# One decoder layer on one core: the last merge's gate blocks as paired half-block products, two groups of copies moved ahead, a shorter head norm

## The chip, the cores and the metric

One of the eight cores of a Trainium2 chip runs the whole program. The metric is the device time of one execution in microseconds; lower is better. TensorE (PE) multiplies, VectorE (DVE) and ScalarE (ACT) do elementwise work, GpSimd (POOL) does a few small steps, SyncE (SP) issues the DMAs.

## What is computed

One layer of a hybrid decoder for 512 prompt tokens and 32 sample tokens (8 sequences of 4), 544 columns in all, with 1024 channels, in float32. Cut to what matters here:

```python
h = rmsnorm(x)
z = h @ w_in                      # conv inputs, q, k, v, o, and three merge gates g_a, g_b, g_c
y_c = (sigmoid(o) * headnorm(mlstm(q, k, v))) @ w_out_c     # 4 heads of 256, RMS norm per head
y_a = (b * dwconv3(c * x_a)) @ w_out_a
y_b = silu(layernorm(dwconv31(glu))) @ w_out_b
u = sigmoid(g_a) * y_a + sigmoid(g_b) * y_b + sigmoid(g_c) * y_c
x = x + u @ w_o
x = x + cross_attention(rmsnorm(x), keys and values of 256 memory tokens)   # p_mem_k, p_mem_v are outputs too
x = x + (silu(gate) * up) @ w_ffn_out
```

## The kernel before

**Numbers in two parts.** Every float32 operand of a large product is split into a rounded high part (ACT copy) and the rest (DVE subtract), `split`, L112; a product is three passes, high by high, high by low and low by high (`PASSES`). Activations lie as channels by tokens in eight tiles of 128 x 544. The 544 columns are worked in two halves of 272 (`HN`), one PSUM bank each.

**Blocks.** `block` makes 128 output channels: for each of the input tiles k, three passes and two halves, so a block of `w_in` with 8 input tiles is 48 matmuls of 128x128 by 272 columns and a block of `w_out_b` with 4 input tiles is 24. The order of TensorE's instructions is the order of the code (`manual_schedule` for PE); on the other engines and on the DMA queue a scheduler orders instructions by a priority, which is their place in the program, PE's instructions counted. `evacuate` moves what it emits 150 places ahead, the weight loads 300 (`PRIO`), `urgent` 600. Weights stream in the order of the list `order`, `ahead` blocks in advance: a DMA to a `wr` buffer (4), a split into a `w` buffer (3).

**Stages.** Queries, keys, values and output gates of the four heads, with the memory's keys and values (`mem_k`, `mem_v`) and the heads' attention put between the matmuls as hooks; then the convolution inputs; then three merges of eight pairs of blocks: gates 68 to 75 with `w_out_c`, 52 to 59 with `w_out_a`, 60 to 67 with `w_out_b` (`merge`, L1038). Then `w_o` and the residual, cross attention, and the feed-forward part. The PSUM has eight banks; `psum(name, mm, s1)` gives mm tiles of two banks and s1 tiles of one.

**The places that the change touches.**
- `merge`: gate block (48 matmuls), Sigmoid into `sg`, `w_out` block (24 matmuls), `sg *= y`, `u[j] += sg`; in the last merge `u[j]` is also split into a pair of an `act` buffer (20 of them).
- `s_pair` (L1483, with `product`, L1474) is how most of the feed-forward part is already done: two blocks of 8 input tiles, taken as a two by two scheme of 512 input channels by 272 columns, come from seven half-block products instead of eight (12 matmuls each) of sums of weights and sums of activations. Its operands are `sA` to `sE` (weights and their sums, `s_emit`) and `b11`, `b2`, `n1t3`, `n2t4` (`b_forms`). Its PSUM tiles `sy` (2), `sz`, `sx` are one bank each.
- `mem_v` (L526): value products of the memory, half by half, into two one-bank tiles that the second half releases by an ACT copy with a scale, `vo`; `mem_rows` (L517) needs a one-bank tile for two transposes (L388).
- `numer` and `finish` (L845, L886): numerator, its sum of squares, and the head norm in [128, 5] columns; POOL makes the power -1/2 (L900); five scalings of `num` (L99) precede the transposes of `head_out` (L911).
- Cross attention: `mqx` and `pm`, zeroed by POOL (L121) when the pool of phase x opens; `xs_t` (L1264) transposes the probabilities and splits them. A pool of a later phase can reuse memory that a closed one has given back.
- `wide_rsqrt` (L346) for the layer norm.

Of the kernel before, what the change touches and what calls it, by code (L numbers as in the profile page):

```python
# [15 lines left out]
P = 128  # L16
# [19 lines left out]
def layer(ctx: ExitStack, tc: tile.TileContext, a):  # L36
# [122 lines left out]
        order += [("in", 4 + c), ("in", 8 + c), ("in", c)]  # L159
    for j in range(8):  # L160
        order += [("in", 52 + j), ("oa", j)]
    for j in range(8):
        order += [("in", 60 + j), ("ob", j)]
    order += [("o", j) for j in range(8)]
    order += [("xq", j) for j in range(8)]
    order += [("xo", j, hf) for hf in range(2) for j in range(8)]
# [21 lines left out]
    def w_emit(key, parts=1):  # L188

        if key[0][0] == "s":  # L190
            with tc.high_priority(PRIO):
                return s_emit(*key)
        if key[0] == "fo":
            return fo_emit(key)
        if key[0] == "v":
            src, n = a["w_v"][key[1], key[2]], 1024
        elif key[0] == "xo":
            n = 512
            src = a["w_xo"][key[1]][:, key[2] * n:(key[2] + 1) * n]
        elif key[0] == "fi":  # L200
            n = 1024
            src = a["w_fi"][key[1]][:, key[2] * n:(key[2] + 1) * n]
        else:
            src = a[src_of[key[0]]][key[1]]
            n = src.shape[-1]
        raw = sb.tile([P, 1024], F32, tag="wr", name=nm("wr"), bufs=4)
        w = sb.tile([P, 2, 1024], F32R, tag="w", name=nm("w"), bufs=3)
        wt[key] = w

        def part(i):  # L210
            c = slice(i * n // parts, (i + 1) * n // parts)
            with tc.high_priority(PRIO if parts == 1 and key not in (("in", 28), ("in", 29)) else 0):
                nc.sync.dma_start(out=raw[:, c], in_=src[:, c])
                split(w[:, 0, c], w[:, 1, c], raw[:, c])
        if parts == 1:
            part(0)
        return part

    def fo_emit(key):

        n = key[3] * P
        with tc.high_priority(PRIO):
            if n > 512:
                raw = sb.tile([P, 1024], F32, tag="wr", name=nm("wr"), bufs=4)
            else:
                raw = sb.tile([P, 512], F32, tag="sraw", name=nm("fr"), bufs=5)
            nc.sync.dma_start(out=raw[:, :n], in_=a["w_ffn_out"][key[1]][:, key[2] * P:key[2] * P + n])
# [117 lines left out]

    def wide_rsqrt(src, n, scale):  # L346

        v, l, y = f1(), f1(), f1()
# [5 lines left out]
        ACT(l[:, :n], v[:, :n], AF.Ln)  # L354
        ACT(y[:, :n], l[:, :n], AF.Exp, scale=-0.5)
# [170 lines left out]
    def mem_v(g, half):  # L526
# [4 lines left out]
        for mb in range(2):  # L531
# [313 lines left out]
    def numer(h, j):  # L845
# [40 lines left out]
    def finish(h):  # L886
# [5 lines left out]
        ACT(n2[:, :NM], num[:NS, 4, :NM], AF.Square, accum_out=ssq[:NS, 4:5])  # L892
# [139 lines left out]
    phase("m")  # L1032
    psum("m", 3, 2)


    u, up_ = [], []

    def merge(g0, kind, ys, first=False, last=False, hooks={}):  # L1038
        for j in range(8):
            if j in hooks:  # L1040
                hooks[j]()
# [11 lines left out]
            if last:
                p = pair()
                split(p[:, 0, :], p[:, 1, :], u[j])
                up_.append(p)
# [396 lines left out]
    def b_forms(k):  # L1453
# [7 lines left out]
        n, m = f1(), f1()  # L1461
        TTo(n[:, :HN], h0[:, :HN], h0[:, HN:], SUB)
        TTo(n[:, HN:], h1[:, HN:], h0[:, HN:], SUB)
        STT(m[:, :HN], n[:, :HN], -1.0, h1[:, HN:], MULT, SUB)
        STT(m[:, HN:], m[:, :HN], -1.0, h1[:, :HN], MULT, SUB)
        for lst, x in ((n1t3, n), (n2t4, m)):
            p = pht([P, 2, T], F32R, tag="bt", bufs=8)
            split(p[:, 0, :], p[:, 1, :], x)
# [5 lines left out]
    def product(ps, w, c, x, first):  # L1474
        for k in range(4):
            for n, (wi, ai) in enumerate(PASSES):
                nc.tensor.matmul(ps, lhsT=w[:, wi, c + k * P:c + (k + 1) * P], rhs=x(k, ai),  # L1477
                                 start=first and k == 0 and n == 0, stop=k == 3 and n == 2, skip_group_check=not first)

    def bank1(tag, bufs):  # L1480
        return ph["ps"].tile([P, HN], F32, tag=tag, name=nm(tag), bufs=bufs)

    def s_pair(f, between):  # L1483

        y, z, x = bank1("sy", 2), bank1("sz", 1), bank1("sx", 1)
        t, u, s = f1(), f1(), f1()
        product(y, wget("sA", f), 0, lambda k, hl: b11[k // 2][:, hl, k % 2, :], True)
        evacuate(lambda: ACT(t[:, :HN], y, AF.Copy))
        wb = wget("sB", f)
        product(z, wb, 512, half(n1t3, 0), True)  # L1490
        evacuate(lambda: ACT(t[:, HN:], z, AF.Copy))

        def p2():
            product(x, wget("sC", f), 0, half(b2, 0), True)
            evacuate(lambda: TTo(u[:, :HN], x, t[:, :HN], ADD))

        if between:
            p2()
        wd = wget("sD", f)
        product(y, wd, 512, half(n2t4, 0), False)  # L1500
        evacuate(lambda: ACT(s[:, :HN], y, AF.Copy))

        def p3():
            product(z, wd, 0, half(b2, 1), False)
            evacuate(lambda: TTo(u[:, HN:], z, s[:, :HN], ADD))

        def p7():
            product(y, wb, 0, half(n1t3, 1), False)
            evacuate(lambda: TTo(t[:, HN:], y, t[:, HN:], ADD))
# [17 lines left out]
    for f in range(22):  # L1527
# [3 lines left out]
                b_forms(k)  # L1531
            continue
        if f == NSTD:
            ph["pstack"].close()
            ph["pstack"] = ExitStack()
            ph["ps"] = ph["pstack"].enter_context(tc.tile_pool(name="ps_g", bufs=1, space=PS, reuse_waits="tile"))
            ph["mm"] = 2
# [191 lines left out]
```

## Time and profile before

| | us |
|---|---|
| median of 3 runs | 1311.2 (1310.02 to 1311.35) |
| the profiled execution | 1310.46 |
| its span, first to last instruction | 1308.5 |
| PE busy | 1287.4 (98%), 10164 matmuls |
| DVE busy | 887.1 (68%) |
| ACT busy | 592.8 (45%) |
| POOL busy | 41.6 (3%) |

The span is what the trace covers; 1.96 us of the execution's time lie outside it. Busy shares are means over stages with different limits; matmuls overlap, so that time per matmul is read from the start of one to the start of another. In a timeline row "[4.69 <-ACT f L107]" means 4.69 us of idle time of that engine just before, ended by that instruction of ACT.

### The profile page before, as it was taken

To read this page: it belongs to the slowest core of one execution; us is meant where nothing else is said; L and a number is where in the kernel's file an instruction comes from. 1 tells how busy PE (TensorE), PEld (TensorE's weight loads), DVE (VectorE), ACT (ScalarE), POOL (GpSimd) and SP (SyncE) were. 2 spreads that over 40 slices of the span, in tenths; PEclk is the share of its full clock that TensorE was granted. 3 is DMA by queue.
4 is the path that set the end of the run, shared out by engine and by line. 5 is a ranking of instruction groups with operands and counts; after the bars stand their busy time and mean duration, and the time that the engine had idled before them with its cause. 6 is when DMAs were issued, how large, how long until landed. Compare 5 with 4: busy or idle time off the path is not lost.

```text
span 1308.5 us, 24803 instructions
## 1 busy us (share of the span) xinstructions
PE 1287.4 (98%) x10164; PEld 1271.9 (97%) x10164; DVE 887.1 (68%) x1486; ACT 592.8 (45%) x1046; POOL 41.6 (3%) x117
## 2 busy tenths in 40 slices
PE   9989999999999999999999999999999999999997
PEld 9989999999999999999999999999999999999997
DVE  6965665655497859976434557886787667777746
ACT  6845545554433222226333446765544444444433
POOL 1000010110010000000000000000000000000000
PEclk9999999999999999999999999999999999999998
DMA  7365644434465233423244224664323233333212
GB/s 262 101 179 172 193 132 137 126 109 148 117 148 168 84 95 82 82 73 89 84 129 147 82 89 144 210 193 142 94 74 113 86 94 109 94 94 94 80 41 69
DMA packets 83265, 155.68 MB, mean 119 GB/s; under 512 B 25124, under 2 KB 33700, under 8 KB 83152
## 3 DMA queue, kind: packets, MB, share of 16 engines
q1 hardware_dynamic: 83152, 154.10, 40.1%
q8 instruction: 80, 1.31, 0.4%
q14 instruction: 33, 0.27, 0.1%
HBM read 137.54 MB, written 16.52 MB: 118 GB/s over the span
## 4 chain that ended last, share of the span: by engine, by line
PE 90%; issue 5%; DVE 2%; ACT 1%; DMA 1%; POOL 0%; SPq 0%; POOLq 0%; DVEq 0%; ACTq 0%
PE mm L110 62%; PE s L110 14%; PE sy L1477 8%; PE sz L1477 4%; PE sx L1477 2%; DVE f L95 0%; ACT w L107 0%; DVE w L95 0%; DMA f<-kscr 0%; ACT act L107 0%; PE s L911 0%; POOL small L381 0%; PE s L827 0%; DMA lt<-in_xT 0%; ACT f L107 0%
## 5 line engine op out<-in xcount | busy, mean ns | idle before, releaser
L110 PE MATMUL mm<-act,w 128*128 128x272 f32 x6336 | 838.0, 289 | 1.9 <-ACT f L107 0.9
L110 PEld LDWEIGHTS mm<-act,w 128*128 128x128 f32 x6336 | 809.7, 189 | 5.1 <-ACT f L107 1.1
L107 ACT ACTIVATE w<-wr 128x1024 fp32r<-128x1024 f32 (+2 forms) x202 | 196.6, 975 | 393.9 <-PE mm L110 229.2
L95 DVE TENSOR_TENSOR w<-wr,w 128x1024 fp32r<-128x1024 f32 (+2 forms) x202 | 225.4, 1116 | 142.7 <-ACT w L107 142.0
L104 DVE SCALAR_TENSOR_TENSOR f<-act,const,f 128x512 f32<-128x512 f32 (+1 forms) x136 | 96.4, 718 | 2.4
L95 DVE TENSOR_TENSOR lt<-mm,lt 128x544 f32<-128x544 f32 x56 | 40.4, 721 | 55.8 <-PE mm L110 55.6
L110 PE MATMUL mm<-act,fw 128*128 128x272 f32 x576 | 76.2, 288 | 0.0
L110 PEld LDWEIGHTS mm<-act,fw 128*128 128x128 f32 x576 | 73.9, 188 | 0.0
L107 ACT ACTIVATE act<-f 128x544 fp32r<-128x544 f32 (+3 forms) x75 | 44.3, 600 | 46.2 <-DVE f L95 40.8
L110 PE MATMUL s<-act,act 128*128 128x256 f32 (+4 forms) x408 | 62.9, 302 | 1.1 <-DVE act L95 0.8
L95 DVE TENSOR_TENSOR act<-f,act 128x544 fp32r<-128x544 f32 (+3 forms) x75 | 48.4, 652 | 20.6 <-ACT act L107 20.3
L95 DVE TENSOR_TENSOR f<-f,f 128x544 f32<-128x544 f32 (+4 forms) x78 | 51.2, 659 | 14.0 <-ACT f L107 12.7
L110 PEld LDWEIGHTS s<-act,act 128*128 128x128 f32 (+1 forms) x408 | 55.0, 184 | 4.2 <-DVE act L95 1.2
L1477 PE MATMUL sy<-bt,w 128*128 128x272 f32 x408 | 56.9, 288 | 0.6 <-ACT f L107 0.6
L1477 PEld LDWEIGHTS sy<-bt,w 128*128 128x128 f32 x408 | 53.3, 188 | 0.8 <-ACT f L107 0.8
L104 DVE SCALAR_TENSOR_TENSOR ct<-ct,wbc,s 128x258 f32<-128x258 f32 x64 | 28.7, 478 | 26.4 <-PE s L110 26.4
L107 ACT ACTIVATE f<-sy 128x272 f32<-128x272 f32 x51 | 19.7, 389 | 39.2 <-PE sy L1477 39.0
L95 DVE TENSOR_TENSOR wr<-wr,wr 128x1024 f32<-128x1024 f32 (+1 forms) x34 | 32.4, 954 | 5.9 <-DMA wr<-in_w_fi 5.5
L95 DVE TENSOR_TENSOR f<-mm,f 128x544 f32<-128x544 f32 (+1 forms) x29 | 20.7, 720 | 22.6 <-PE mm L110 20.4
L107 ACT ACTIVATE fw<-fr 128x512 fp32r<-128x512 f32 x26 | 16.4, 632 | 42.9 <-PE mm L110 41.6
L107 ACT ACTIVATE f<-mm 128x544 f32<-128x544 f32 (+1 forms) x50 | 30.5, 611 | 6.1 <-PE mm L110 5.9
L95 DVE TENSOR_TENSOR xpair<-kr,xpair 128x512 fp32r<-128x512 f32 x46 | 30.5, 681 | 3.5 <-ACT xpair L107 3.4
(237 smaller groups left out, 1405.5 us busy)
## 6 DMA issues: line engine op xcount, KB each, us to landing
wr<-in_w_in SPq DMA_DIRECT2D x74, 512.0 KB, 3.7
wr<-in_w_fi SPq DMA_DIRECT2D x44, 512.0 KB, 3.6
ct<-in_ctn SPq DMA_DIRECT2D x32, 258.0 KB, 3.0
out_sct<-ct SPq DMA_DIRECT2D x32, 258.0 KB, 3.3
kr<-in_ktc SPq DMA_DIRECT2D x32, 256.0 KB, 3.8
kr<-in_vc SPq DMA_DIRECT2D x32, 256.0 KB, 3.9
fr<-in_w_ffn_out SPq DMA_DIRECT2D x32, 256.0 KB, 2.7
lt<-in_xT SPq DMA_DIRECT2D x16, 272.0 KB, 3.7
```

The source lines that it names most:

```text
L95: nc.vector.tensor_tensor(out=out, in0=x, in1=y, op=op)
L104: nc.vector.scalar_tensor_tensor(out=out, in0=x, scalar=s, in1=y, op0=op0, op1=op1)
L107: nc.scalar.activation(out, x, f, **kw)
L110: nc.tensor.matmul(out, lhsT=l, rhs=r, start=start, stop=stop)
L1477: nc.tensor.matmul(ps, lhsT=w[:, wi, c + k * P:c + (k + 1) * P], rhs=x(k, ai), start=first and k == 0 and n == 0, stop=k == 3 and n == 2, ...
```

## The change

Six edits. (1) The eight gate blocks of the last merge become four pairs of seven products; the weights 60 to 67 are laid out by pair on the host (`w_gt`), their sums are made on DVE as those of the feed-forward part, the activations' sums in `h_forms`, called in the merge before. The products' code moves to `seven`, shared with `s_pair`. The PSUM is switched to the layout of the feed-forward part before this merge. (2) The `vo` copies of `mem_v` go through `evacuate`. (3) So does `xs_t`. (4) The head norm has fewer steps. (5) The zeros of `mqx` and `pm` are written by ACT. (6) `wide_rsqrt` works in place.

```diff
-    for j in range(8):
-        order += [("in", 60 + j), ("ob", j)]
+    for p in range(4):
+        f = 100 + p
+        order += [("sA", f), ("sB", f), ("sC", f), ("sD", f), ("ob", 2 * p), ("ob", 2 * p + 1), ("sE", f)]
...
+            src = a["w_fi"][f] if f < 100 else a["w_gt"][f - 100]
...
-        if key[0] == "fo":
+        if key[0] in ("fo", "ob"):
             return fo_emit(key)
...
-                ACT(vo, ps, AF.Copy, scale=mst["rm"][:, mb:mb + 1])
+                evacuate(lambda: ACT(vo, ps, AF.Copy, scale=mst["rm"][:, mb:mb + 1]))
...
-        ACT(np_[:, :NM], np_[:, :NM], AF.Square, accum_out=ssq[:, j:j + 1])
+        ACT(np_[:, :NM], np_[:, :NM], AF.Square, scale=1.0 / 16, accum_out=ssq[:, j:j + 1])
...
-        nc.vector.reciprocal(dd, dd)
-        TTo(xx, ssq, dd, MULT)
-        TTo(xx, xx, dd, MULT)
-        TS(xx, xx, 1.0 / NM, MULT, EPS, ADD)
+        STT(xx, dd, EPS, dd, MULT, MULT)
+        STT(xx, xx, 1e-37, ssq, MAX, ADD)
         nc.gpsimd.tensor_tensor(out=rs, in0=xx, in1=nhalf, op=ALU.pow)
-        TTo(rs, rs, dd, MULT)
...
+    def seven(f, b, u, t, s, l1, l2):
+        b11, b2, n1t3, n2t4 = b
+        y, z, x = bank1("sy", 2), bank1("sz", 1), bank1("sx", 1)
+        product(y, wget("sA", f), 0, b11, True)
+        evacuate(lambda: ACT(t[:, :HN], y, AF.Copy))
+        wb = wget("sB", f)
+        product(z, wb, 512, half(n1t3, 0), True)
+        evacuate(lambda: ACT(t[:, HN:], z, AF.Copy))
...
+        product(y, wd, 512, half(n2t4, 0), False)
+        evacuate(lambda: ACT(s[:, :HN], y, AF.Copy))
...
+        for g in [p3, *l1, p7, *l2] if l1 else [p2, p7, p3]:
+            g()
+        product(y, wget("sE", f), 0, half(n2t4, 1), False)
+        return y
...
+    def h_forms(k):
+        h, n = act_t([P, 2, T], F32), act_t([P, 2, T], F32)
+        for i in range(2):
+            x = hT[k + 4 * i].bitcast(F32)
+            TTo(h[:, i, :], x[:, 0, :], x[:, 1, :], ADD)
+        for lst, p in zip(hx[2:], sums_of(h[:, 0, :], h[:, 1, :], n[:, 0, :], n[:, 1, :], h)):
+            lst.append(p)
+    def merge2(f0, kind, ys):
+        for p in range(4):
+            g, t, s = f1(), f1(), f1()
...
+            def add(j, sg):
+                TTo(sg, pv(py[j % 2]), sg, MULT)
+                TTo(u[j], u[j], sg, ADD)
+                q = pair()
+                split(q[:, 0, :], q[:, 1, :], u[j])
+                up_.append(q)
+            def y0():
+                evacuate(lambda: ACT(g, g, AF.Sigmoid))
+                py.append(block((kind, 2 * p), ys))
+                add(2 * p, g)
+            y = seven(f0 + p, hx, g, t, s, [y0], [lambda: py.append(block((kind, 2 * p + 1), ys))])
+            ACT(s[:, HN:], t[:, HN:], AF.Sigmoid, scale=-1.0)
+            evacuate(lambda: ACT(s[:, :HN], y, AF.Sigmoid, scale=-1.0))
+            add(2 * p + 1, s)
...
-    merge(52, "oa", ya, hooks={1: ln_sum, 2: ln_mean, 4: ln_var})
-    merge(60, "ob", yb, last=True)
+    merge(52, "oa", ya, hooks={1: ln_sum, 2: ln_mean, 3: lambda: h_forms(0), 4: ln_var, 5: lambda: h_forms(1),
+                               6: lambda: h_forms(2), 7: lambda: h_forms(3)})
+    psum7("ps_p")
+    ahead[0] = 4
+    merge2(100, "ob", yb)
+    ahead[0] = 2
...
-    MS(mqx, 0.0)
-    for x in pm:
-        MS(x, 0.0)
+    for x in (mqx, *pm):
+        ACT(x.rearrange("p a (n c) -> p (a n) c", c=64), ones32[:, 0:64].rearrange("p (o c) -> p o c", o=1)
+            .to_broadcast([P, 18, 64]), AF.Copy, scale=0.0)
...
-        return (lambda: evacuate(f)) if t[0] in "to" else f
+        return (lambda: evacuate(f)) if t[0] in "toT" else f
```

`sums_of` makes the two sums `n` and `m` of one input tile's halves (one DVE instruction on 544 columns or two on 272, then two on 272) and splits both into `bt` buffers (8, in the phase's pool); `psum7` is the switch that the feed-forward part already made.

## Rows read from the trace of the kernel before

**Rows 1.** The page's busy times: engine, busy us (share of the span), instructions
```profile
PE 1287.4 (98%) x10164; PEld 1271.9 (97%) x10164; DVE 887.1 (68%) x1486; ACT 592.8 (45%) x1046; POOL 41.6 (3%) x117
```
**Rows 2.** PE's waits, longest first: us in total, times, longest
```profile
PE s L388 <- ACT f L107: 4.7, 1, 4.7
PE s L911 <- DVE num L99: 1.6, 1, 1.6
```
**Rows 3.** The chain that ended last: start us, us, what
```profile
586.28 18.08 PE mm L110 x144
...
1104.82 3.01 PE sy L1477 x24
...
1121.38 3.01 PE sy L1477 x24
```
**Rows 4.** Busy time by stage: stretch, us, PE, PEld, DVE, ACT, POOL, clock, DMA
```profile
594.00:641.00 47.00, 47.00 (x377) 47.00 (x376) 25.63 (x36) 24.65 (x31) 0.00 (x0) 1.00 0.30 87
641.00:712.00 71.00, 71.00 (x568) 71.00 (x567) 30.47 (x39) 22.70 (x31) 0.00 (x0) 1.00 0.39 123
```
**Rows 5.** Timeline, DVE: the kinds of instruction that the new operands need
```profile
588.73 2.52 DVE L104 SCALAR_TENSOR_TENSOR f<-s,f 128x272 f32<-128x272 f32 x7
...
612.92 2.75 DVE L95 TENSOR_TENSOR f<-f,f 128x544 f32<-128x544 f32 x4
...
1000.48 1.23 DVE L95 TENSOR_TENSOR wr<-wr,wr 128x1024 f32<-128x1024 f32 x1 [1.29 <-DMA wr<-in_w_fi]
```
**Rows 6.** Timeline, PE: the two switches of the PSUM in the feed-forward part
```profile
989.84 1.78 PE L1477 MATMUL sy<-bt,w 128*128 128x272 f32 x12 [0.56 <-ACT f L107]
...
1272.54 2.63 PE L110 MATMUL s<-act,fw 128*128 128x288 f32 x18 [0.55 <-ACT f L107]
```
**Rows 7.** Timeline around PE's longest wait, all engines
```profile
70.74 0.66 ACT L107 ACTIVATE ph<-f 4x544 fp32r<-4x544 f32 x1 [1.93 <-DVE f L648]
...
71.32 1.21 DVE L95 TENSOR_TENSOR w<-wr,w 128x1024 fp32r<-128x1024 f32 x1
...
74.53 1.23 DVE L95 TENSOR_TENSOR w<-wr,w 128x1024 fp32r<-128x1024 f32 x1 [0.83 <-ACT w L107]
...
75.52 0.45 ACT L107 ACTIVATE f<-s,const 128x256 f32<-128x256 f32 x1
...
76.02 0.43 PE L388 MATMUL s<-const,const 128*128 128x128 f32 x2 [4.69 <-ACT f L107]
...
83.53 0.91 PE L110 MATMUL mm<-act,w 128*128 128x272 f32 x6
```
**Rows 8.** Stretches right after that wait, columns as in rows 4
```profile
76.00:77.60 1.60, 1.58 (x9) 1.58 (x10) 0.18 (x1) 0.83 (x3) 0.00 (x0) 0.65 0.45 95
77.60:79.00 1.40, 1.40 (x9) 1.40 (x8) 0.00 (x0) 0.08 (x1) 0.00 (x0) 0.50 0.91 105
79.00:81.00 2.00, 2.00 (x15) 2.00 (x15) 0.00 (x0) 0.54 (x2) 0.00 (x0) 0.77 0.94 352
```
**Rows 9.** Timeline around the last head's norm; last, line L99 by itself (ns minimum/median/maximum)
```profile
389.02 0.15 DVE L95 TENSOR_TENSOR small<-small,small 128x5 f32<-128x5 f32 x1
...
389.81 0.16 DVE L101 TENSOR_SCALAR small<-small 128x5 f32<-128x5 f32 x1
...
391.68 3.05 POOL L121 MEMSET ph<- 128x1152 f32 x3
...
392.49 3.42 DVE L99 TENSOR_SCALAR num<-num,small 128x256 f32<-128x256 f32 x5
...
395.02 1.02 PE L911 MATMUL s<-const,num 128*128 128x128 f32 x4 [1.64 <-DVE num L99]
...
L99 DVE TENSOR_SCALAR num<-num,small x5: 335/342/2383, 392.5 to 395.6; 128x256 f32<-128x256 f32 x4, 32x256 f32<-32x256 f32 x1
```
**Rows 10.** Timeline, cross attention: PE's first products with the probabilities
```profile
799.01 0.50 PE L110 MATMUL s<-act,act 128*128 128x512 f32 x1 [0.25 <-ACT act L107]
...
800.35 2.12 PE L110 MATMUL s<-act,act 128*128 128x512 f32 x8 [0.84 <-DVE act L95]
```

More of the change, by code (lines that the diff above doesn't have):

```diff
@@ L219, in fo_emit @@
     def fo_emit(key):
-        n = key[3] * P
+        n, c = (key[3] * P, key[2] * P) if key[0] == "fo" else (512, 0)
+        src = a["w_ffn_out"] if key[0] == "fo" else a[src_of[key[0]]]
         with tc.high_priority(PRIO):
@@ L226, in fo_emit @@
                 raw = sb.tile([P, 512], F32, tag="sraw", name=nm("fr"), bufs=5)
-            nc.sync.dma_start(out=raw[:, :n], in_=a["w_ffn_out"][key[1]][:, key[2] * P:key[2] * P + n])
+            nc.sync.dma_start(out=raw[:, :n], in_=src[key[1]][:, c:c + n])
             if n > 512:
@@ L242, in s_emit @@
             r = [sb.tile([P, 1024], F32, tag="wr", name=nm("wr"), bufs=4) for _ in range(2)]
+            src = a["w_fi"][f] if f < 100 else a["w_gt"][f - 100]
             for i in range(2):
-                nc.sync.dma_start(out=r[i], in_=a["w_fi"][f][:, i * 1024:(i + 1) * 1024])
+                nc.sync.dma_start(out=r[i], in_=src[:, i * 1024:(i + 1) * 1024])
             sraw_[f] = r
@@ L346, in wide_rsqrt @@
     def wide_rsqrt(src, n, scale):
-        v, l, y = f1(), f1(), f1()
+        v, y = f1(), f1()
         if isinstance(src, list):
@@ L353, in wide_rsqrt @@
             TS(v[:, :n], src, scale, MULT, EPS, ADD)
-        ACT(l[:, :n], v[:, :n], AF.Ln)
-        ACT(y[:, :n], l[:, :n], AF.Exp, scale=-0.5)
+        ACT(y[:, :n], v[:, :n], AF.Ln)
+        ACT(y[:, :n], y[:, :n], AF.Exp, scale=-0.5)
         t = f1()
@@ L891, in finish @@
         TTo(num[:NS, 4, :], nps[0:32, :], n2, ADD)
-        ACT(n2[:, :NM], num[:NS, 4, :NM], AF.Square, accum_out=ssq[:NS, 4:5])
+        ACT(n2[:, :NM], num[:NS, 4, :NM], AF.Square, scale=1.0 / 16, accum_out=ssq[:NS, 4:5])
         dd, xx, rs = small([P, 5]), small([P, 5]), small([P, 5])
@@ L1033, in layer, with half, product, bank1 @@
     psum("m", 3, 2)
+    def half(lst, hf):
+        return lambda k, hl: lst[k][:, hl, BANK[hf]]
+    def product(ps, w, c, x, first):
+        for k in range(4):
+            for n, (wi, ai) in enumerate(PASSES):
+                nc.tensor.matmul(ps, lhsT=w[:, wi, c + k * P:c + (k + 1) * P], rhs=x(k, ai),
+                                 start=first and k == 0 and n == 0, stop=k == 3 and n == 2, skip_group_check=not first)
+    def bank1(tag, bufs):
+        return ph["ps"].tile([P, HN], F32, tag=tag, name=nm(tag), bufs=bufs)
@@ new lines, in psum7, with sums_of @@
+    def psum7(name):
+        ph["pstack"].close()
+        ph["pstack"] = ExitStack()
+        ph["ps"] = ph["pstack"].enter_context(tc.tile_pool(name=name, bufs=1, space=PS, reuse_waits="tile"))
+        ph["mm"], ph["s1"] = 2, 0
+    def sums_of(h0, h1, n, m, h=None):
+        if h is None:
+            TTo(n[:, :HN], h0[:, :HN], h0[:, HN:], SUB)
+            TTo(n[:, HN:], h1[:, HN:], h0[:, HN:], SUB)
+        else:
+            q = h.rearrange("p i (a n) -> p (i a) n", n=HN)
+            TTo(n.rearrange("p (a n) -> p a n", n=HN), q[:, 0::3, :], q[:, 1:2, :].to_broadcast([P, 2, HN]), SUB)
+        STT(m[:, :HN], n[:, :HN], -1.0, h1[:, HN:], MULT, SUB)
+        STT(m[:, HN:], m[:, :HN], -1.0, h1[:, :HN], MULT, SUB)
+        r = []
+        for x in (n, m):
+            p = pht([P, 2, T], F32R, tag="bt", bufs=8)
+            split(p[:, 0, :], p[:, 1, :], x)
+            r.append(p)
+        return r
@@ new lines, in seven, with p2, p3, p7 @@
+    def seven(f, b, u, t, s, l1, l2):
[6 more added lines that the diff above has]
+        evacuate(lambda: ACT(t[:, HN:], z, AF.Copy))
+        def p2():
+            product(x, wget("sC", f), 0, half(b2, 0), True)
+            evacuate(lambda: TTo(u[:, :HN], x, t[:, :HN], ADD))
+        if l1:
+            p2()
+        wd = wget("sD", f)
+        product(y, wd, 512, half(n2t4, 0), False)
+        evacuate(lambda: ACT(s[:, :HN], y, AF.Copy))
+        def p3():
+            product(z, wd, 0, half(b2, 1), False)
+            evacuate(lambda: TTo(u[:, HN:], z, s[:, :HN], ADD))
+        def p7():
+            product(y, wb, 0, half(n1t3, 1), False)
+            evacuate(lambda: TTo(t[:, HN:], y, t[:, HN:], ADD))
+        for g in [p3, *l1, p7, *l2] if l1 else [p2, p7, p3]:
+            g()
+        product(y, wget("sE", f), 0, half(n2t4, 1), False)
+        return y
@@ L1036, in layer, with merge @@
     u, up_ = [], []
-    def merge(g0, kind, ys, first=False, last=False, hooks={}):
+    def merge(g0, kind, ys, first=False, hooks={}):
         for j in range(8):
@@ L1052, in merge @@
                 TTo(u[j], u[j], sg, ADD)
[L1053 to L1056, printed above, removed]
+    hx = [lambda k, hl: hT[k][:, hl, :HN], hT[4:], [], []]
+    def h_forms(k):
[8 more added lines that the diff above has]
+            g, t, s = f1(), f1(), f1()
+            py = []
+            def add(j, sg):
[12 more added lines that the diff above has]
+            add(2 * p + 1, s)
     ycp = []
@@ L1460, in b_forms @@
         b2.append(ga_split(h1))
[L1461 to L1468, printed above, removed]
-            lst.append(p)
-    def half(lst, hf):
-        return lambda k, hl: lst[k][:, hl, BANK[hf]]
@@ L1474, in product @@
[L1474 to L1481, printed above, removed]
+        for lst, p in zip((n1t3, n2t4), sums_of(h0, h1, f1(), f1())):
+            lst.append(p)
@@ L1483, in s_pair @@
+    bx = (lambda k, hl: b11[k // 2][:, hl, k % 2, :], b2, n1t3, n2t4)
     def s_pair(f, between):
-        y, z, x = bank1("sy", 2), bank1("sz", 1), bank1("sx", 1)
         t, u, s = f1(), f1(), f1()
[L1487 to L1509, printed above, removed]
         n = len(between) // 2
-        for g in [p3, *between[:n], p7, *between[n:]] if between else [p2, p7, p3]:
-            g()
@@ L1514, in s_pair @@
-        product(y, wget("sE", f), 0, half(n2t4, 1), False)
+        y = seven(f, bx, u, t, s, between[:n], between[n:])
         ACT(s[:, HN:], t[:, HN:], AF.Silu, scale=-1.0)
@@ L1533, in layer @@
         if f == NSTD:
[L1534 to L1537, printed above, removed]
+            psum7("ps_g")
         ga[f] = s_pair(f, [part(fo, key) for key in fo_in[f]])
@@ L1675 @@
         A[n] = _blocks(g[n][0])
+    b = A["w_in"][60:68].reshape(4, 2, P, 2, 512)
+    A["w_gt"] = np.stack([b[:, 0, :, 0], b[:, 1, :, 1], b[:, 0, :, 1], b[:, 1, :, 0]], axis=2).reshape(4, P, 2048)
     b = _blocks(g["w_ffn_in"][0]).reshape(2, 22, P, 2, 512)
```

## The prediction

> **What bounds the kernel now.** I read the page's busy times first, then PE's waits, then the chain that ended last and the timelines around the places the change touches. TensorE is busy for 98% of the span and VectorE for 68% [rows 1]: a change pays where it takes matmuls away or closes a hole in PE's stream, and work put on DVE, ACT or POOL costs only where PE comes to wait for it. Of the holes, two lie where the change works: 4.7 us before two transposes of line 388 that waited for ACT, and 1.6 us before line 911, which waited for the scaling of `num` on DVE [rows 2]. Two smaller ones lie in cross attention [rows 10]. In the merges PE runs without a hole, 144 matmuls in 18.08 us, 125.6 ns each [rows 3].
>
> **Edit 1, the seven products.** A pair of gate blocks with its two `w_out` blocks is 2 x 48 + 2 x 24 = 144 matmuls, 18.08 us [rows 3]. After it is 7 x 12 + 2 x 24 = 132. The feed-forward part already runs this very sequence (seven products, 48 matmuls between): from one pair to the next it is 1121.38 - 1104.82 = 16.56 us, any waits included [rows 3]. So 1.52 us per pair and 6.08 for four go from PE, and all of it is on the path, since PE is what ends this stage.
>
> The price per matmul can be put to a rule. The row has 125.6 ns for 272 columns [rows 3]; the Trainium skill (TensorE: Matmul & The Clock Gate, Back-to-back issue gap) gives a warm gap of columns / 2.4 + 2.5 ns, an estimate of 115.8 ns here. By that page the 48 matmuls would bring 5.56 us and the total would come out 0.5 us higher; the row's price is used.
>
> What it adds, and what hides it. `h_forms` costs DVE five instructions of 544 columns at 0.69 us and two of 272 at 0.36 per tile [rows 5], 4.2 us, 16.7 for four, and ACT two copies each (some 0.66 by a copy of as many columns [rows 7]), 5.3 in all. The stretch of the merge with `w_out_a` from the first hook on has 47.0 - 25.6 = 21.4 us of free DVE time [rows 4], and `hT` has long been there, so these sums may also run before their hook. Each pair's weights want three sums (1.23 + 0.69 + 0.69) and 1536 more columns to split (about 1.85), and three evacuations of 272 columns (1.1): some 5.6 us of DVE per pair on top of 16.56 x 30.47 / 71 = 7.1 [rows 4], so 12.7 of 16.56. It fits, as it does in the feed-forward part. If this cover failed, PE would wait at the second product for the last `n1t3` or for a weight sum; that is a rival below. The DMAs stay the same bytes; `w_out_b` moves from the `wr` to the `sraw` buffers, where the cross attention's key tiles were loaded early. Those, and the zeros of `mqx` and `pm`, must now wait until the `bt` buffers are given back, at the end of this merge; the `w_o` stage, with 48 matmuls x 8 = 48 us, lies between that and their first use. I cost this at nothing; bound above: one key tile late, about the 1.2 us of a hole like those of rows 10.
>
> **Two switches of the PSUM.** The change adds one on the way in and moves the one on the way out, where the first `w_o` block takes the banks of `sy` and so waits for the last Sigmoid. Neither is in the trace; the nearest rows are the two switches of the feed-forward part, of the same tiles, 0.56 and 0.55 us of waiting [rows 6]. I take these, +1.11, and keep 0 and 2.5 us (each with a DVE or ACT instruction in front) as ends.
>
> **Edits 4 and 5, the head norm.** In the last head's norm each small step costs its slot in DVE's queue, 389.81 - 389.02 = 0.79 us, since a convolution tap comes in between [rows 9]. The edit takes two steps from before POOL's power and one from behind it. And one of the five scalings took 2383 ns where its fellows take 342: it lay beside POOL's three memsets of 3.05 us [rows 9], which edit 5 takes off POOL (ACT writes them instead, three instructions in the `w_o` stage, where nobody waits for them). Either part alone moves the end by about 2 us, PE waits for 1.64: that wait goes, and no more than it, -1.64. Bounds: 0 (taps or other work fill the slots) and -1.64. In heads 1 to 3 nobody waited [rows 2].
>
> **Edit 2, the value sums.** PE stood 4.69 us before line 388: the transposes of `mem_rows` need a one-bank tile that the `vo` copies release, and the first copy ran at 75.52, after ACT had done the gates' chain that began at 70.74 [rows 7]. ACT was free for 1.93 us before that. Counted along the program, some 125 instructions (60 matmuls of the output-gate blocks, 24 and 12 to 24 of the values, loads and splits) lie between the chain's last ACT instructions and the two copies, and the edit moves the copies 150 ahead: they come to stand before the chain's end. So I expect them in that free time. What is late next: the transposes run at 71.33; the next value product needs its weights' low part, which DVE ends at 71.32 + 1.21 = 72.53; its 24 matmuls take 3.0 us, to 75.6; the next weights end at 74.53 + 1.23 = 75.76 [rows 7]; another 24 matmuls, some 2.9 us, to 78.66. Before, that point was 83.53 [rows 7]: -4.87. Part of this is the clock: after the hole the granted clock was 0.65, 0.50 and 0.77 over 5.0 us [rows 8], that is partly at 1.2 GHz, worth 1.6 x 0.35 + 1.4 x 0.50 + 2.0 x 0.23 = 1.7 us; the new waits, 1.2 and 0.2 us, are too short to be like it. Bounds: 0 (the order of ACT stays as it was) and 4.69 + 1.7 = -6.4. I take -4.87, since each of its dates is a row.
>
> **Edit 3, the probabilities.** In front of the first products with them PE waited 0.25 and 0.84 us for their splits [rows 10], which lay behind other work on ACT and DVE. Moved ahead: -1.09, bounds 0 and -1.1. **Edit 6** saves a buffer, no time.
>
> **Sum.** -6.08 + 1.11 - 1.64 - 4.87 - 1.09 = -12.57 on the profiled execution of 1310.46 us gives 1297.9. The median of the runs is 0.74 above that execution: 1298.6 us.
>
> **Rivals.**
> - *The value sums stay where they are.* The scheduler orders ACT by when it thinks things are ready; if it thinks the products late, a higher place changes nothing. For it: ACT's own order let the copies stand behind the chain, although it had nothing to do for 1.93 us [rows 7]. Against it: the count above. Then edit 2 does not do what it says: 1298.6 + 4.9 = 1303.5. Chance 0.23.
> - *DVE is the bound in the last merge.* Its free time in the merge before is 21.4 us for 16.7 of sums and the first pair's weights, about 4.5 more; if the sums run late, and each pair's weight sums and splits (1.23 + 0.69 + 1.23 behind each other) come 1.5 us late as well, 4 x 1.5 us are lost and the products' gain with them: 1298.6 + 6 = 1304.6. Against it: the feed-forward part's even 16.56 us. Chance 0.13.
> - *Slower: the 20 `act` buffers run out.* In the last merge they hold 8 of `hT`, 4 of the layer norm, 2 more of `u` per pair, and sA, sC, sE: 15, 17, 19, 21. It decides if PE meets the limit a pair early, because `h_forms`'s two or the previous operands are still held. Then an operand can be split only when a product gives one back (ACT 0.66, DVE 0.69 and handing over, 1.7 us each), and the raw buffers it holds delay the next pair's loads; 3 x 1.7 us per pair and about 7 for two loads is 12 us a pair, for two pairs 24, with the clock's 1.7 us after each hole as in rows 8: 1298.6 + 24 + 3.4 = 1326. Against it: only the fourth pair is over by one, and sA comes free after one product. Chance 0.04.
>
> **The numbers.** The forecast gets 0.57, the rivals 0.23, 0.13 and 0.04, the rest (0.03) is unforeseen order. About 0.2% (2.6 us) is what a measurement of this kernel can tell from no change; the first three cases all lie beyond it, so faster 0.92, same 0.04, slower 0.04. The low end takes the favourable bounds, switches at nothing and the clock's share in full: 1298.6 - 1.1 - 1.5 = 1296.0. The high end takes the first two rivals with the switches' upper end: 1304.6 + 1.4 = 1306.0.
>
> **What would show it.** Pairs of 16.56 us in the last merge, 66 us in all; waits of about half a microsecond at its two ends; `vo` copies on ACT before 71 us and no clock below 1.0 from 71 to 81; no wait at line 911; no scaling of `num` above 0.4 us. Wrong if PE waits for `bt` or `w` inside the last merge, if the wait before line 388 still has over 4 us, or if the time won before 400 us is lost again to a wait for DVE that the earlier PE uncovers.

## The result, and the profile after

| | before | after |
|---|---|---|
| median, us | 1311.01 (4 runs) | 1301.7 (4 runs, 1301.45 to 1302.94) |
| profiled execution, us | 1310.46 | 1301.55 |
| its span, us | 1308.5 | 1299.8 |
| PE busy, us | 1287.4 | 1281.0 |
| DVE busy, us | 887.1 | 920.7 |

The ratio of the times is 0.9932 (95% interval 0.9915 to 0.9949). The kernel became 9.3 us faster; 12.6 were forecast, 12.57 by the sum. Set beside the profiled executions, 1301.55 stands against 1297.9: **3.65 us are missing**, and PE's waits show one entry that was in no term at such a size. The page's busy times [rows 1] and then PE's waits [rows 2] of the changed kernel (us in total, times, longest):

```profile
PE 1281.0 (99%) x10116; PEld 1266.4 (97%) x10116; DVE 920.7 (71%) x1538; ACT 612.6 (47%) x1085; POOL 38.4 (3%) x114
```
```profile
PE sz L1042 <- DVE bt L95: 4.0, 1, 4.0
...
PE s L110 <- DVE w L95: 0.9, 2, 0.7
...
PE s L1404 <- DVE f L99: 0.2, 1, 0.2
```

The 4.7 us of ACT and the 1.6 us of `num` are gone. In their place PE waits once for 4 us, for a `bt`, that is for one of the activation sums of edit 1.

**Where the forecast came true.** The timeline of the changed kernel around the former hole [rows 7], then around the head norm [rows 9], then PE's last product of two of the four pairs, and the way out of the merge:

```profile
70.57 0.84 ACT L107 ACTIVATE f<-s,const 128x256 f32<-128x256 f32 x2 [1.88 <-DVE f L651]
...
71.10 0.43 PE L391 MATMUL s<-const,const 128*128 128x128 f32 x2
...
72.47 2.90 PE L110 MATMUL s<-w,act 128*128 128x256 f32 x22 [0.70 <-DVE w L95]
...
75.77 2.90 PE L110 MATMUL s<-act,w 128*128 128x256 f32 x22 [0.16 <-DVE w L95]
...
78.51 0.91 PE L110 MATMUL mm<-act,w 128*128 128x272 f32 x6
...
383.88 1.39 DVE L99 TENSOR_SCALAR num<-num,small 128x256 f32<-128x256 f32 x5 [1.08 <-POOL small L902]
...
388.21 0.60 PE L912 MATMUL s<-const,num 128*128 128x128 f32 x4
...
654.12 1.68 PE L1042 MATMUL sy<-bt,act 128*128 128x272 f32 x12
...
670.70 1.68 PE L1042 MATMUL sy<-bt,act 128*128 128x272 f32 x12
...
706.10 1.15 PE L110 MATMUL mm<-act,w 128*128 128x272 f32 x7 [0.55 <-ACT f L107]
```

The copies run at 70.57, in ACT's former free time, and the two waits that were to be late next stand there with 0.70 and 0.16 us. The granted clock is 1.00 from 71 to 81 us. The transposes of `num` follow the scalings without a wait, pairs end 16.58 us apart (654.12 to 670.70), and the way out costs 0.55 us.

**Where it did not.** The way into the merge, DVE, ACT and PE from 629 to 644; then the same place by stretches (us; PE, PEld, DVE, ACT and POOL busy; clock; DMA):

```profile
629.73 1.35 DVE L95 TENSOR_TENSOR act<-act 128x544 f32<-128x544 f32 x2
...
633.21 0.64 ACT L107 ACTIVATE bt<-act 128x544 fp32r<-128x544 f32 x1
633.42 1.67 PE L1042 MATMUL sy<-act,act 128*128 128x272 f32 x12
...
634.93 1.42 PE L1042 MATMUL sz<-bt,w 128*128 128x272 f32 x10
635.28 1.21 DVE L95 TENSOR_TENSOR wr<-wr,wr 128x1024 f32<-128x1024 f32 x1
...
637.55 0.68 DVE L95 TENSOR_TENSOR wr<-wr,wr 128x512 f32<-128x512 f32 x1
638.15 1.21 DVE L95 TENSOR_TENSOR w<-wr,w 128x1024 fp32r<-128x1024 f32 x1
...
639.64 0.71 DVE L95 TENSOR_TENSOR bt<-act,bt 128x544 fp32r<-128x544 f32 x1
...
640.40 0.82 PE L1042 MATMUL sz<-bt,w 128*128 128x272 f32 x2 [4.05 <-DVE bt L95]
...
641.02 2.76 PE L1042 MATMUL sx<-act,act 128*128 128x272 f32 x12
```
```profile
636.50:640.40 3.90, 0.00 (x0) 0.00 (x1) 3.90 (x6) 1.06 (x1) 0.00 (x0) 0.95 0.39 128
640.40:641.80 1.40, 1.40 (x6) 1.40 (x7) 1.31 (x3) 1.07 (x3) 0.00 (x0) 0.50 0.81 205
641.80:643.60 1.80, 1.80 (x10) 1.80 (x10) 0.98 (x2) 0.17 (x1) 0.00 (x0) 0.54 0.37 146
```

The last tile's sums begin at 629.73. The second product needs one of them, `n`, in its two parts. The rounded part is ACT's copy at 633.21, done at 633.85; what is late is a single DVE instruction, the rest of that split, which runs at 639.64. In between DVE is never idle: it makes weights, those of pair 0, and among them, between 635.28 and 639.3, three instructions (1.21, 0.68 and 1.21 us) for pair 1's `sB`, which PE wants at 657. The second product has done 10 of its 12 matmuls and stands. After the hole the granted clock is 0.50 and 0.54 over 3.2 us, that is 1.2 GHz for most of it, and the third product takes 2.6 us from its first matmul to the next product's where others take 1.5; 1.4 x 0.50 + 1.8 x 0.46 = 1.5 us of full speed are lost there. So the entry costs 4.05 + 1.5 = 5.5 us in this trace.

### The profile page after: what moved, and what is told of

It reads as the page before. It is cut to its first block, busy times and chain, and to the rows that moved or that the text cites. A ratio compares the mean times of both kernels' runs of the same rounds, so it can differ in the third digit from the quotient of the medians.

```text
span 1299.8 us, 24777 instructions
## 1 busy us (share of the span) xinstructions
PE 1281.0 (99%) x10116; PEld 1266.4 (97%) x10116; DVE 920.7 (71%) x1538; ACT 612.6 (47%) x1085; POOL 38.4 (3%) x114
## 4 chain that ended last, share of the span: by engine, by line
PE 48%; DVE 3%; ACT 1%; issue 1%; POOLq 0%; DVEq 0%; ACTq 0%
PE mm L110 25%; PE sy L1042 9%; PE s L110 6%; PE sz L1042 5%; PE sx L1042 2%; DVE act L95 1%; DVE w L95 1%; DVE wr L95 0%; DVE f L95 0%; ACT f L107 0%; ACT act L107 0%; DVE bt L95 0%; ACT w L107 0%; PE s L1374 0%; DVE lt L95 0%
## 5 line engine op out<-in xcount | busy, mean ns | idle before, releaser
L110 PE MATMUL mm<-act,w 128*128 128x272 f32 x5760 | 765.8, 290 | 1.9 <-ACT f L107 1.5
L110 PEld LDWEIGHTS mm<-act,w 128*128 128x128 f32 x5760 | 737.7, 189 | 4.8 <-ACT f L107 1.9
L110 PE MATMUL mm<-act,fw 128*128 128x272 f32 x768 | 101.7, 288 | 0.0
L110 PEld LDWEIGHTS mm<-act,fw 128*128 128x128 f32 x768 | 98.6, 188 | 0.0
L1042 PE MATMUL sy<-bt,w 128*128 128x272 f32 x504 | 70.3, 288 | 0.6 <-ACT f L107 0.6
L1042 PEld LDWEIGHTS sy<-bt,w 128*128 128x128 f32 x504 | 65.9, 188 | 0.8 <-ACT f L107 0.8
L95 DVE TENSOR_TENSOR f<-f,f 128x544 f32<-128x544 f32 (+4 forms) x78 | 51.3, 659 | 14.1 <-ACT f L107 12.8
L95 DVE TENSOR_TENSOR wr<-wr,wr 128x1024 f32<-128x1024 f32 (+1 forms) x42 | 40.1, 954 | 5.3 <-DMA wr<-in_w_fi 4.9
L1042 PE MATMUL sz<-bt,w 128*128 128x272 f32 x252 | 35.7, 290 | 4.0 <-DVE bt L95 4.0
L95 DVE TENSOR_TENSOR act<-wr,act 128x512 fp32r<-128x512 f32 x61 | 39.2, 685 | 0.6 <-ACT act L107 0.6
L1042 PEld LDWEIGHTS sz<-bt,w 128*128 128x128 f32 x252 | 33.3, 189 | 4.3 <-DVE bt L95 4.3
```

Of the source, the lines that this page charges most:

```text
L95: nc.vector.tensor_tensor(out=out, in0=x, in1=y, op=op)
L110: nc.tensor.matmul(out, lhsT=l, rhs=r, start=start, stop=stop)
```

## Experiments

All edits are to the changed kernel unless said otherwise. Times of single runs of one kernel scatter by 1 to 4 us, so that a single run can't show what a small edit is worth. Two sources of the scatter stand in the traces. PE's `mm` products just before the value sums (at 70.42 in the kernel before, at 70.31 in the changed one) start anywhere from 69.6 to 70.4 us in kernels whose programs are the same up to there; and after the same wait the clock stays low for longer in some traces than in others. So it helps to compare lengths of stages, from one landmark of the traces to the next: these `mm` products; the first `mm` products after the value sums; the Sigmoid of one block on ACT; a place in the `w_o` stage where PE waits 0.16 us; the end of the span. Two of the landmarks in the kernel before, then in the changed one (timeline of ACT; the chain that ended last):

```profile
418.07 0.61 ACT L107 ACTIVATE f<-mm 128x544 f32<-128x544 f32 x1
...
762.87 4.04 PE mm L110 x31
```
```profile
410.64 0.61 ACT L107 ACTIVATE f<-mm 128x544 f32<-128x544 f32 x1
...
755.49 4.04 PE mm L110 x31
```

| length of the stage, us | value sums | to the Sigmoid | to the `w_o` stage, with the last merge | to the end |
|---|---|---|---|---|
| before | 13.1 | 334.5 | 344.8 | 545.6 |
| changed | 8.2 | 332.1 | 344.9 | 544.3 |
| changed, last tile's sums urgent (1) | 8.2 | 332.1 | 341.2 | 543.9 |
| changed without edit 1 (4) | 8.2 | 332.9 | 344.8 | 544.3 |
| changed without edit 2 (5) | 14.1 | 332.1 | 345.9 | 544.0 |
| changed without edit 3 (5) | 8.2 | 332.1 | 346.2 | 545.3 |
| changed without edit 4 (6) | 8.2 | 332.1 | 346.2 | 544.0 |
| before with edit 5 alone (6) | 14.2 | 332.1 | 344.8 | 545.3 |
| before with edit 4 alone (6) | 13.1 | 333.9 | 344.8 | 547.1 |

In the changed kernel without edit 3 and in the one without edit 4 the last merge has the same wait of 4.05 us and takes 1.3 us more: the granted clock is 0.50 to past 645 us there, and only to about 643 in the changed kernel's trace. The way into the merge so costs from 5.5 to 6.8 us.

**1. Is it the order of DVE's work, or too much of it?** Two ways to get the sums done earlier: in `urgent`, 600 places ahead instead of none (the weights have 300), or one block earlier in the merge.

```diff
-                               6: lambda: h_forms(2), 7: lambda: h_forms(3)})
+                               6: lambda: h_forms(2), 7: lambda: urgent(lambda: h_forms(3))})
```


> The last tile's sums stay in the last block, but 600 places ahead in the order. Order: they pass the weight work that is not yet needed, wait 0 to 0.6 us, 1297.7 to 1298.2 us. Amount: the weight work is late in their place, PE waits 2 to 4 us for a w tile instead of bt, 1300 to 1302 us.

Measured: 1297.93 us median (1297.5 to 1298.41), ratio to before 0.9905 [0.989, 0.992]. PE's way in:

```profile
634.66 1.77 PE L1042 MATMUL sy<-act,act 128*128 128x272 f32 x12 [1.28 <-ACT f L107]
636.26 1.67 PE L1042 MATMUL sz<-bt,w 128*128 128x272 f32 x12
...
640.55 0.90 PE L1042 MATMUL sy<-bt,w 128*128 128x272 f32 x5 [0.24 <-DVE bt L95]
```

One tile's place in the order is worth 3.8 us, with the same instructions on every engine: the granted clock stays at 1.00, and the way in still waits 1.28 and 0.24 us. What is late next is the Sigmoid of gate 59 on ACT, for which the first product waits. This version beats both kernels.

```diff
-    merge(52, ..., hooks={1: ln_sum, 2: ln_mean, 3: lambda: h_forms(0), 4: ln_var, 5: lambda: h_forms(1),
-                               6: lambda: h_forms(2), 7: lambda: h_forms(3)})
+    merge(52, ..., hooks={1: ln_sum, 2: lambda: (ln_mean(), h_forms(0)), 3: lambda: h_forms(1), 4: ln_var,
+                               5: lambda: h_forms(2), 6: lambda: h_forms(3)})
```


> The changed kernel waits 4.05 us in the last merge's second product for the last tile's sums. Theory (order): DVE has the time, but the last tile's sums are called in the last block before they are needed and stand on DVE behind weight sums and splits that are 300 places ahead, partly for the second pair. With the calls one block (9 us) earlier the wait falls to the 0 to 0.6 us of the switch: 1297.7 to 1298.2 us against 1301.7. Rival (amount): DVE has too much to do in this stretch, so the wait stays within 1 us of 4: 1301 to 1302 us.

Measured: 1306.51 us (8 runs), ratio 0.9971 [0.996, 0.9981], so worse than the change itself, against the expectation. DVE and PE at the switch:

```profile
636.18 1.23 DVE L95 TENSOR_TENSOR w<-wr,w 128x1024 fp32r<-128x1024 f32 x1
637.31 0.44 DVE L104 SCALAR_TENSOR_TENSOR act<-act,act 128x272 f32<-128x272 f32 x1
...
639.57 0.73 DVE L95 TENSOR_TENSOR f<-mm,f 128x544 f32<-128x544 f32 x1
...
640.44 3.06 PE L1042 MATMUL sy<-act,act 128*128 128x272 f32 x12 [7.54 <-DVE f L95]
```

The last tile's sums are again behind the weights (637.31): one block of program is less than the 300 places that the weights are ahead. PE now stands before the first product, and the trace puts that on `sg *= y` of the last block, at 639.57, behind the same weights.

**2. Both of those, and the two of the merge moved too.** In the merge, the Sigmoid and `sg *= y` go through `evacuate`; the expectations below call that 3000 places, but the constant is 150, half of what the weights have.

```diff
-            ACT(sg, pv(pg), AF.Sigmoid)
+            evacuate(lambda: ACT(sg, pv(pg), AF.Sigmoid))
...
-                TTo(sg, pv(py), sg, MULT)
+                evacuate(lambda: TTo(sg, pv(py), sg, MULT))
```
With the earlier sums:

> The sums one block earlier each (as in forms_early, 1306.5 us, with a wait of 7.54 us for the bank of the last block of the merge), plus the sigmoid and the multiplication moved 3000 places forward. If the 7.54 us came from the one multiplication that frees the bank and stood behind the weights of pairs 0 and 1, the wait falls to under 1 us and the time to 1297 to 1298.5 us, the same as with urgent sums. Rival: the earlier sums themselves cost time in the merge before (buffers that are taken earlier, a VectorE that is fuller), and the time stays at 1303 or more even if the wait at the switch is gone.

Measured: 1302.03 us, ratio 0.9941 [0.9926, 0.9956]. The 7.5 us are gone, but the wait for the sums is back:

```profile
PE sz L1042 <- DVE bt L95: 4.1, 1, 4.1
```

`sg *= y` of the last block runs hardly earlier here (638.76) and the first product starts on time, at 633.47. In the changed kernel it runs at 640.62, again after that product has started. So that product does not need this instruction's bank in every order; why it did in forms_early stays open.

With the last tile urgent:

> The changed kernel with the last tile's sums urgent (as in forms_urgent), and besides that the merge's sigmoid on ScalarE and its multiplication of the gate with y on VectorE moved 3000 places forward in the priority list (the same helper that the evacuations of the products use), so that no preparation of weights or of the gates' inputs may stand in front of them. The theory of the order (what the first products wait for is always the instruction that was sorted behind work needed later) expects that the 1.28 us before the first product, which waited for the sigmoid of gate 59, falls to 0.3 or less, that the multiplication ends before the second product, and so 1296.7 us in fast runs (1296.2 to 1297.6). Rival: ScalarE and VectorE simply have too much to do in the 10 us before the switch, whatever the order; then the wait moves to another operand (a weight of pair 0 or the last tile's splits) and the time stays at 1297.5 to 1298.5.

Measured: 1305.27 us, ratio 0.9963 [0.9951, 0.9976]: 7 us worse than the urgent sums alone. PE's waits:

```profile
PE sz L1042 <- DVE bt L95: 6.4, 2, 5.7
```

The trace has the tile before the last in the place where the last one was: its sums, which have no lead, end after 640 us. With that one urgent as well:

> As forms_urgent_evac (sigmoid and multiplication of the merge 3000 places forward), but with the sums of the last two tiles urgent instead of the last one alone. The theory of the order, as it stands after forms_urgent_evac: VectorE was not short of time there, the tile before the last had become the one that was sorted behind the weights of pairs 0 and 1, so the 6.4 us belong to that tile's place alone. In the instruction order of this kernel all the sums' splits stand before the weight sums of pair 1. It expects that no wait for sums is left at the switch (under 0.3 us), at most 1.3 us for the sigmoid or for pair 0's first weights, and 1296.5 to 1298.2 us. Rival: the merge's last blocks hold more work for VectorE and ScalarE than fits, so what is put forward pushes something else back that the first products need (a weight of pair 0, or a bank), and 3 us or more are waited for at the switch: 1300 us or more.

Measured: 1300.57 us, ratio 0.9926 [0.9912, 0.9939]. No wait for sums is left, and 2.9 us for ACT (0.73 and 2.19) are there in their place. PE, DVE and ACT:

```profile
633.69 1.76 PE L1042 MATMUL sy<-act,act 128*128 128x272 f32 x12 [0.73 <-ACT f L107]
...
637.94 1.22 DVE L95 TENSOR_TENSOR wr<-wr,wr 128x1024 f32<-128x1024 f32 x1
...
639.25 1.06 ACT L107 ACTIVATE w<-wr 128x1024 fp32r<-128x1024 f32 x1 [2.49 <-DVE wr L95]
...
640.22 0.38 ACT L107 ACTIVATE f<-sy 128x272 f32<-128x272 f32 x1
...
640.65 1.86 PE L1042 MATMUL sy<-bt,w 128*128 128x272 f32 x12 [2.19 <-ACT f L107]
```

ACT stood 2.49 us at the copy of pair 1's sum, which waits for DVE, and behind it in ACT's queue stood the copy of the first product, which must have read `sy` before the fourth product is added there. The rival of this run was right: in this trace DVE is never idle from 622 to 643 us, and what was put forward pushed something else back. The order decides which of the late items PE meets; only forms_urgent hit one that costs little.

**3. The weights' distance.** The changed kernel with `ahead` left at 2.

```diff
-    ahead[0] = 4
     merge2(100, "ob", yb)
```


> The changed kernel with one thing undone: the weights are prepared two entries of the order ahead in the last merge, as everywhere else, and not four. The theory of the order expects that pair 1's weight sums (two of 1.21 us on VectorE) no longer run in front of the last tile's sums, so the wait of the second product falls from 4.05 us to about 1.6 us (4.05 less 2 x 1.21); against that, sums that are started two entries later may be late for their products, up to 1 us a pair. So 1299.3 us if nothing new is late, up to 1303 if each pair waits. Rival: pair 0's own weights (needed for the same pair, whatever the distance) are what stands in front; then the wait stays between 3 and 4 us and the time at 1301 to 1302 or above.

Measured: 1312.76 us (10 runs), ratio 1.0021 [1.0012, 1.0031]; slower than the kernel before the change. PE's waits:

```profile
PE sz L1042 <- DVE bt L95: 3.8, 1, 3.8
PE sy L1042 <- DVE w L95: 2.8, 3, 1.0
PE sy L1042 <- ACT w L107: 2.3, 3, 0.8
```
```profile
659.50 0.52 PE L1042 MATMUL sx<-act,act 128*128 128x272 f32 x2 [0.26 <-ACT act L107]
...
679.50 0.52 PE L1042 MATMUL sx<-act,act 128*128 128x272 f32 x2 [0.25 <-ACT act L107]
```

Two entries of the list are less than the weights' 300 places: pair 1's `sB` still runs in front of the last tile's sums, so the wait at the entry stays within the rival's 3 to 4 us, though not for its reason alone, since pair 0's own weights are only part of what stands in front. And pairs 1 to 3 now find the operands `sC` and `sD` late, and a pair takes 20.0 us (659.50 to 679.50) where it took 16.58: 3 x 3.4 = 10.3 us. The price of 1 us a pair was far too low.

**4. Edit 1 undone, all else kept** (full blocks 60 to 67, no switch on the way in, no `h_forms`).

> Edit 1 undone, all others kept. If edit 1 brought 6.08 less the 4.05 and 0.55 of its two waits, that is 1.5 us, this takes 1301.7 + 1.5 = 1303.2 us. Rival: the unsplit forecast of edit 1 (5.0 us net) is hidden somewhere else: 1306 to 1307 us. No wait of over 0.3 us between 390 and 760 us.

Measured: 1302.41 us (1301.35 to 1303.94), ratio 0.994 [0.9925, 0.9955], against 0.9932 [0.9915, 0.9949] with the edit. As made, the seven products bring next to nothing: the stage takes 344.8 us without them and 344.9 with them. With the urgent sums the kernel takes 1302.41 - 1297.93 = 4.5 us less than without edit 1. The stage itself is 3.6 us shorter (344.8 to 341.2), not the 4.97 of the sum, mostly since the way in still waits 1.5 us there instead of 0.56. Another 0.7 us lie before the Sigmoid, where the kernel without edit 1, against its expectation, has a wait of 0.49 us at 396.92 for DVE's convolution.

**5. Edits 2 and 3 undone, one at a time** (one run each).

```diff
-                evacuate(lambda: ACT(vo, ps, AF.Copy, scale=mst["rm"][:, mb:mb + 1]))
+                ACT(vo, ps, AF.Copy, scale=mst["rm"][:, mb:mb + 1])
```


> Edit 2 undone, all others kept. Theory: the copies stand at 75 us again behind the gates' chain, a wait of 4.7 us before the two transposes, the clock below 1.0 after it, 5.0 us more than the changed kernel: 1306.7 us. Rival: the copies stay early because of the new order of everything else: 1301.7 us.

Measured: 1307.55 us. The hole is back, with its clock; PE and ACT, then two stretches after it:

```profile
74.51 0.45 ACT L107 ACTIVATE f<-s,const 128x256 f32<-128x256 f32 x1
...
75.02 0.69 PE L391 MATMUL s<-const,const 128*128 128x128 f32 x2 [4.69 <-ACT f L107]
```
```profile
75.50:77.00 1.50, 1.50 (x9) 1.50 (x9) 0.00 (x0) 0.38 (x1) 0.00 (x0) 0.50 0.40 101
77.00:78.50 1.50, 1.50 (x9) 1.50 (x9) 0.00 (x0) 0.20 (x1) 0.00 (x0) 0.50 0.83 213
```
The value sums take 14.1 us instead of 8.2. In the kernel before they took 13.1, with the same wait of 4.69 us but fewer microseconds at the low clock after it. So the edit is worth 4.9 to 6 us, by how long the clock stays low.

```diff
-        return (lambda: evacuate(f)) if t[0] in "toT" else f
+        return (lambda: evacuate(f)) if t[0] in "to" else f
```


> Edit 3 undone, all others kept. Theory: the two waits of 0.25 and 0.84 us in front of the first products with the probabilities are back and the new one of 0.24 us is gone: 0.85 us more, 1302.5 us. Rival: they do not come back, since the key tiles of the cross attention are split at other times now: 1301.7 us.

Measured: 1303.35 us, one wait of 0.84 us back, the 0.24 us before L1404 gone: the edit is worth 0.6 us by its waits. The 1.65 us of the run are no measure of it, as 1.3 of them lie in the last merge, in the clock after a wait that both kernels have. From the `w_o` stage to the end it is 545.3 against 544.3 us, so about 1 us.

**6. Edits 4 and 5, each alone** (one run each). The long norm in the changed kernel, that is edit 5 without edit 4:

```diff
-        STT(xx, dd, EPS, dd, MULT, MULT)
-        STT(xx, xx, 1e-37, ssq, MAX, ADD)
+        nc.vector.reciprocal(dd, dd)
+        TTo(xx, ssq, dd, MULT)
+        TTo(xx, xx, dd, MULT)
+        TS(xx, xx, 1.0 / NM, MULT, EPS, ADD)
         nc.gpsimd.tensor_tensor(out=rs, in0=xx, in1=nhalf, op=ALU.pow)
+        TTo(rs, rs, dd, MULT)
```


> Edit 4 undone, all others kept (zeros by ACT, after the last merge). If either part alone is enough, no wait before the last head's transposes: 1301.7 us. If the steps made the wait: up to 1.6 us more, 1303.3 us.

Measured: 1302.14 us, and no wait before the transposes; the stage up to the Sigmoid takes 332.1 us, as with edit 4. In the kernel before the change, the zeros by ACT alone:

> The kernel before with edit 5 alone (ACT writes the zeros; the norm has all its steps). If either part alone is enough, all five scalings take 0.33 to 0.36 us and the wait is gone: some 1309.4 us. Rival: the steps alone make the wait, so it stays at over 1 us with scalings of normal length.

Measured: 1308.13 us, where a run of the kernel before beside it took 1308.75; the five scalings take 334 to 346 ns each, and the stage up to the Sigmoid falls from 334.5 to 332.1 us, by 2.4. And the short norm alone:

> The kernel before with edit 4 alone (shorter head norm; POOL still writes the zeros). If either part alone is enough, the wait before line 911 (1.64 us) is gone though one scaling still takes over 2 us beside the memsets: 1.6 us less than before, some 1309.4 us. Rival: the collision with the memsets alone makes the wait, so it stays at over 1 us.

Measured: 1310.55 us, span 1308.5, that is nothing. The scalings and POOL's zeros, PE some ten microseconds later, and PE in cross attention, in this kernel:

```profile
388.54 3.06 POOL L121 MEMSET ph<- 128x1152 f32 x3
...
388.62 4.16 DVE L99 TENSOR_SCALAR num<-num,small 128x256 f32<-128x256 f32 x5 [1.08 <-POOL small L898]
...
403.31 16.94 PE L110 MATMUL mm<-act,w 128*128 128x272 f32 x133 [1.57 <-DVE lt L104]
...
798.76 0.50 PE L110 MATMUL s<-act,act 128*128 128x512 f32 x1 [1.42 <-ACT act L107]
```
The wait before the transposes goes, but 1.57 us are waited for at 403, for DVE's convolution, so that 0.6 us are left at the Sigmoid (333.9 against 334.5). In cross attention PE then waits 1.42 us for the probabilities, where it waited 0.25 [rows 10], and nothing is left at the end. Edit 5 alone brings the whole 2.4 us; beside it edit 4 brings nothing.

## Why the forecast was right in sign and 3.65 us too low

The median, 1301.7 us, lies inside the range that was stated, 1296.0 to 1306.0. Step by step, with what the traces measured along PE's path:

- **Value sums, forecast -4.87.** The first `mm` product after them starts at 78.51, where it was 83.53 [rows 7]: -5.02, of which 0.11 were there before the value sums, so -4.91. Each of the dates came true within 0.25 us, the copies' place in ACT's order above all, and with it the rival that left them in place fell.
- **Head norm, -1.64.** The mechanism (a scaling beside POOL's zeros) was right, two details were not. "Either part alone moves the end by about 2 us" holds for the transposes, but of edit 4's gain most was given back at 403 and the rest in cross attention. And the hole was a little larger than its row: the first four transposes took 1.02 us [rows 9] and take 0.60, as each waited for its scaling. By 411 us the kernel is 7.43 us ahead (the Sigmoid of one block that ACT ran at 418.07 runs at 410.64), of which 5.02 were there after the value sums, which leaves 2.4.
- **Pairs, -6.08.** 4 x (18.08 - 16.58) = 6.0. Right, at 16.58 / 132 = 125.6 ns a matmul, the row's price. By the formula that the Trainium skill (TensorE: Matmul & The Clock Gate, Back-to-back issue gap) gives for an isolated matmul it would be an estimate of 115.8 ns and a pair 15.3 us, which no pair shows. The cover within the pairs held. What it rests on is `ahead` = 4: with 2 the second rival, late weight sums, comes at 3.4 us a pair.
- **Way out, +0.55.** 0.55.
- **Way in, +0.56.** This is the step that failed, together with "It fits", by which `h_forms` has no term in the sum: 4.05 us of waiting and 1.5 us of clock, 5.5 in all. The working compared amounts: 21.4 us of free DVE time for 16.7 of sums. It hoped that the sums "may also run before their hook". Only tile 0's began before it, at 586.86, by less than 2 us. PE passes the other three hooks at about 606, 615 and 624 (a pair of blocks every 9.04 us, counted back from 633.42), and their sums begin at 615.45, 624.08 and 629.73, the last 3.7 us before the first product; DVE had its gaps before, the last of them at 613, and none from there until it waits for the third product. And it put the first pair's weights at 4.5 us without asking where in the queue they stand: all weights are 300 places ahead, which reaches into pair 1 with `ahead` at 4 and at 2, and so work that is needed 17 us later stood in front of an operand that was needed at once. That is the first half of the rival "DVE is the bound in the last merge"; its price there, 6 us for late sums and four late pairs, was spread over the wrong places.
- **Probabilities, -1.09.** The waits fell from 0.25 + 0.84 to 0.24. From the `w_o` stage to the end the kernel takes 1.3 us less, nearly all of it in cross attention: the last residual of the `w_o` stage is 7.4 us earlier (762.00 to 754.62) and one at the end of cross attention 8.6 (901.50 to 892.88). Undoing the edit costs 1.0 of this.

Summed along the path: -5.0 - 2.4 for the two early ones, then for the last merge -6.0 + 0.55 + 5.5 = 0.1, and -1.3 from there to the end: -8.6, where the span went from 1308.5 to 1299.8, that is -8.7. That forms_urgent's profiled run took 1297.5 us, where the sum gave 1297.9, is in part luck: its way in still waits 1 us longer than forecast, and the head norm's hole gives 0.8 us more.

## What to carry to other kernels

Free time of an engine is not cover by itself: name the last instruction that the consumer needs and what the queue holds in front of it, prefetches above all, which have a lead in the order whether or not they are urgent. Where an engine is full up to a switch, moving one thing forward pushes another back: the first move won 3.8 us here, and those added to it lost part of that or more. Look at which of the late items costs least, and run each order, since of five tried here two were worse than the change itself, two can't be told from it and one is better. Sums put several blocks earlier, into the gaps that DVE had before 613 us, were not tried. To tell what a small edit is worth, compare the lengths of stages in the traces, as whole runs differ by more. A distance of prefetch that looks too long at one place (4 entries) may be what a later place lives on.

## What was not expected of the hardware

A one-input DVE instruction beside POOL's zeros of 128x1152 was held for about the whole zero run, not slowed by a share: one scaling took 2383 ns [rows 9], and 3126 ns in the kernel with the short norm alone, against 342 ns. Each ended some 0.15 us after the third of the memsets of 1.06 us (at 394.87 and 391.75), though one began 0.8 us and the other 0.1 us into the run of zeros. The convolution taps, with two inputs, took 0.75 us beside the zeros (at 391.83 in the kernel before) as without them (at 389.14). The Trainium skill (SBUF — State Buffer, SBUF: two separate sides) has both: VectorE's two-port forms and GpSimd lock a pair of ports against each other for a whole instruction, and a two-input instruction is in this only where GpSimd's reads SBUF, which zeros don't. These rows agree in that the tap is free and the scaling stands; that the scaling runs in such a form is not shown by a run, nor why it stood past the end of one memset.
